# Half of the partial sums of three chunks: from an add on VectorE to a copy on ScalarE and an accumulating transfer

## The chip, the cores and the metric

The kernel runs on one core of a Trainium2 chip. The metric is the device time of one execution in microseconds; the time before is 965.22 us, the median of three runs (965.08 to 965.33). A profile was taken of one further execution of the same kernel. In views of the profile PE is TensorE (matmuls), PEld its weight load, DVE is VectorE, ACT ScalarE, POOL GpSimd and SP SyncE; an engine's name with a q is its queue, where transfers are issued.

## The reference

One encoder layer on 512 tokens of width 2048, all in float32. The part that matters here is the normalisation with a shift and a scale that depend on `c`, and the wide input projection:

```
mod = silu(c) @ w_ada + b_ada                  # 2048 -> 3 * 2048: shift, scale, gate
h = rms_norm(x, g) * (1 + scale) + shift       # 512 x 2048
proj = h @ w_in                                # 2048 -> 7168 columns
# proj is split into q, k, v, z of 8 attention heads and of 4 retention heads;
# attention (three dilated windows mixed), retention in both directions,
# both gated by silu(z), concatenated to y
out = rms_norm(x + gate * (y @ w_out), final_gain)
```

## The kernel before, in words

Every float32 product is made of three matmuls: each operand is split into a high part (a rounded copy, `hh` for h, `whi` for weights) and a low part (`hl`, `wlo`: the rest), and `mm3` (L89 to L92) adds high times high, low times high and high times low in PSUM. Of each piece of weights, ScalarE makes the high part (L173) and VectorE subtracts to get the low part (L178).

The input projection is cut into units of 256 columns. The shift and scale of a k tile (128 of the 2048 rows of h) need a full pass over 256 columns of `w_ada`, and that pass is long, so the first 13 units (phase 1) are not computed one after the other over all sixteen k tiles. The k tiles come in six chunks of 1, 2, 2, 3, 4 and 4 (`CHUNKS`, L36), and each chunk is multiplied into all 13 units as soon as its part of h is there. Two units (0 and 1) keep their PSUM banks (`pp`) through all chunks. The other eleven are "loose": in each chunk, each gets two banks `pw` of a pool of three (`psA`), and when its matmuls of this chunk are done, `post` (L945) takes the two banks out. The first time a unit is taken out, ScalarE copies the banks to the sums `acc` in SBUF (L952). Each later time VectorE adds them: `acc = acc + pw`, one instruction for each of the two banks (L954). The order of the units is turned round from chunk to chunk, and the last loose unit of a chunk keeps its banks and goes on as the first one of the next, so it isn't taken out at the turn. In chunks two, three and four that leaves 9, 10 and 10 units that are added.

Beside this, the next chunk's h is prepared in pieces (`ada_pieces`, L209): SP loads a block of `w_ada` (`araw`, three buffers, L223), VectorE adds it, weighted with silu(c), to `aacc` (L234; ScalarE does the first, L230), TensorE transposes the sum into a bank `psm` (L262), ScalarE adds it up along the row (`junk`, L267), three tiny VectorE instructions make shift and scale (L269 to L271), ScalarE makes `hh` and a float32 copy `ht` (L189, L193), and VectorE makes `hl` (L202). The pieces are handed out between the items of the current chunk. An item is loaded and converted ahead of its matmuls (`LEAD1` = 8 items for the load, `LOOK` = 2 for the conversion, three buffers each for `whi` and `wlo`). Weights and `w_ada` blocks are both issued by SP, in one queue. The first item of the later work on GpSimd is an iota at L491.

Each engine works its own list in order. The last chunk's `hh` tiles (k = 12 to 15) are made in chunk five; before that their SBUF is not used.

Of the kernel before, what the change touches and what calls it, by code (L numbers as in the profile page):

```python
# [9 lines left out]
F32 = mybir.dt.float32  # L10
F32R = mybir.dt.float32r
I32 = mybir.dt.int32
AF = mybir.ActivationFunctionType
ALU = mybir.AluOpType
# [3 lines left out]
P = 128  # L18
D = 2048
S = 512  # L20
NT = S // P
NK = D // P
# [13 lines left out]
CHUNKS = [1, 2, 2, 3, 4, 4]  # L36
# [14 lines left out]
def trunk_kernel(ctx, tc, x, c, norm_gain, w_ada, b_ada, w_in, w_out, dec_f, dec_b, final_gain, out):  # L51
    nc = tc.nc
# [10 lines left out]
    def bank(pool, nm):  # L63
        return pool.tile([P, 512], F32, tag="b", name=nm)
# [30 lines left out]
    c_row = const.tile([NK, P], F32, name="c_row")  # L95
    hp_scope = ExitStack()
    hp = hp_scope.enter_context(tc.tile_pool(name="hp", bufs=1, side="right"))
    hh = [hp.tile([P, S], F32R, name=f"hh{k}") for k in range(NK)]

    groups = [range(sum(CHUNKS[:i]), sum(CHUNKS[: i + 1])) for i in range(len(CHUNKS))]  # L100
    xt_tiles = {i: hp.tile([P, len(g), S], F32, tag=f"g{i}", name=f"xT{i}") for i, g in enumerate(groups) if i}
# [83 lines left out]

    def make_h(k, nk, k_first):
        tmp = aap.tile([P, S], F32, tag="ht", name="ht", bufs=4)
        a, b = av[:, k : k + 1], sv[:, k : k + 1]
        nc.scalar.activation(hh[k], xT[k], AF.Identity, scale=a, bias=b)  # L189
        if k_first == 1:  # L190
            nc.vector.tensor_scalar(tmp, xT[k], a, b, op0=ALU.mult, op1=ALU.add)
        else:
            nc.scalar.activation(tmp, xT[k], AF.Identity, scale=a, bias=b)  # L193
        tmps[k] = tmp
# [11 lines left out]
    def h_pieces(k0, nk):  # L206
        return [(lambda f=f, k=k: f(k, nk, k0)) for f in (make_h, make_hl) for k in range(k0, k0 + nk)]
# [350 lines left out]
    def shared_conv(c0s, k0, nk):  # L558
        m = len(c0s)
        lo_c = min(c0s)  # L560
        st = {}

        def ld():
            if k0 == 0 and lo_c == FIRST_W:
                assert m == 2
            elif "raw" not in st:
                raw = raw_tile()
                rv = raw[:, : nk * m * UC].rearrange("p (k f) -> p k f", k=nk)
                nc.sync.dma_start(
                    rv,  # L570
                    wi[k0 * P : (k0 + nk) * P, lo_c : lo_c + m * UC].rearrange("(k p) f -> p k f", p=P),
                )
                st["raw"] = rv

        def cv(j):
            off = (c0s[j] - lo_c) // UC
            if nk == 1:
                if k0 == 0 and lo_c == FIRST_W:
                    st[0] = first_w
                if off // 2 not in st:  # L580
                    a, b = off // 2 * 512, min(off // 2 * 512 + 512, m * UC)
                    st[off // 2] = conv(st["raw"][:, 0, a:b], b - a)
                w = st[off // 2]
                o = off % 2 * UC
                return w[0][:, o : o + UC], w[1][:, o : o + UC]
            return conv(st["raw"][:, :, off * UC : (off + 1) * UC], nk * UC)

        return [(ld, lambda j=j: cv(j)) for j in range(m)]
# [32 lines left out]
    def flush():  # L621
        while loaded or pending:
            feed(None)

    def unit_items(mode, c0, k0, nk, pss, start, stop, post, cvf=None):
        items = []
        hold = {}
        ks = list(range(k0, k0 + nk))
        for a in range(0, nk, 2):
# [16 lines left out]
            def mm(wt, kk=kk, last=(a + 2 >= nk)):  # L646
                if "ps" not in hold:
                    hold["ps"] = pss()
                ps = hold["ps"]
                wh = wt[0].rearrange("p (k f) -> p k f", f=UC)  # L650
                wl = wt[1].rearrange("p (k f) -> p k f", f=UC)
                if mode == "T":
                    for ft in range(2):
                        fs = slice(ft * P, (ft + 1) * P)
                        for j, k in enumerate(kk):
                            mm3(
                                ps[ft], wh[:, j, fs], wl[:, j, fs], hh[k], hl[k],
                                start and k == k0, stop and k == k0 + nk - 1, k == 0,
                            )
                else:  # L660
                    for t in range(NT):
                        o = ps[t // 2][:, (t % 2) * UC : (t % 2 + 1) * UC]
                        ts = slice(t * P, (t + 1) * P)
                        for j, k in enumerate(kk):
                            mm3(
                                o, hh[k][:, ts], hl[k][:, ts], wh[:, j, :], wl[:, j, :],
                                start and k == k0 and t % 2 == 0, stop and k == k0 + nk - 1,
                            )
                if last:
                    post(ps)  # L670
# [211 lines left out]
    def heads(g):  # L882
        return attention(2 * g, 0) + attention(2 * g + 1, 1)
# [6 lines left out]
    accs = {}  # L890
    begun = set()
    keep_now = {}
# [13 lines left out]
    def plan(fs, start, span):  # L906
        for i, f in enumerate(fs):
            agenda.setdefault(start + (i * span) // len(fs), []).append(f)
# [7 lines left out]
    def feed_next(item):  # L916
        nonlocal fed
        feed(item)
        fed += 1
        for f in agenda.pop(fed - 1, ()):  # L920
            f()

    for ci, nk in enumerate(CHUNKS):
        lastc = ci == len(CHUNKS) - 1
        early["on"] = ci < len(CHUNKS) - 2
        items = []
        order = ORDER
        if (len(CHUNKS) - 1 - ci) % 2:
            order = order[::-1]
        if lastc:  # L930
            order = list(range(NU))
        cvs = {}
        if nk <= 2:
            for g in GROUPS:
                per = 4 // nk
                for i in range(0, len(g), per):
                    part = g[i : i + per]
                    for u, f in zip(part, shared_conv([ph1[u][1] for u in part], k0, nk)):
                        cvs[u] = f
        loose = [u for u in order if u >= N_PERSIST]  # L940
        kept, keep_now = keep_now, {} if lastc else {loose[-1]: None}
        for u in order:
            mode, c0, ev = ph1[u]

            def post(ps, u=u, ev=ev, lastc=lastc, keep_now=keep_now):  # L945
                if u in keep_now:
                    keep_now[u] = ps
                    return
                if u >= N_PERSIST:
                    for i in range(2):  # L950
                        if u not in begun:
                            nc.scalar.copy(accs[u][i], ps[i])  # L952
                        else:
                            nc.vector.tensor_tensor(accs[u][i], accs[u][i], ps[i], op=ALU.add)  # L954
                    begun.add(u)
                if lastc:
                    src = accs[u] if u >= N_PERSIST else ps
                    if u < 4:
                        ev(src)
                    else:  # L960
                        queue.append(lambda: ev(src))
                    if u % 4 == 3:
                        queue.extend(heads(u // 4))

            if u < N_PERSIST:
                pss = lambda u=u: persist[u]
                start, stop = ci == 0, lastc
            elif u in kept:
                pss = lambda u=u, kept=kept: kept[u]
                start, stop = False, u not in keep_now  # L970
            else:
                pss = lambda: [bank(psA, "pw") for _ in range(2)]
                start, stop = True, u not in keep_now
            items += unit_items(mode, c0, k0, nk, pss, start, stop, post, cvs.get(u))
        if not lastc:
            n2 = CHUNKS[ci + 1]
            nxt = []
            for i in range(0, n2, 4):
                nxt += ada_pieces(k0 + nk + i, min(4, n2 - i))
            before_last = ci == len(CHUNKS) - 2  # L980
            span = int(len(items) * ADA_SPAN) if before_last else len(items)
            plan(nxt, fed + LAG, span)
            if before_last:
                agenda.setdefault(fed + LAG + span, []).append(open_wk)
        if ci == 0:
            for it in items:
                it["load"]()
        for it in items:
            feed_next(it)
        k0 += nk  # L990
# [299 lines left out]
    for t in range(NT):  # L1290
        ts = slice(t * P, (t + 1) * P)
        ps = bank(psP, "po")[:, :256]
# [30 lines left out]
```

## Time and profile before

| what | value |
|---|---|
| median of three runs | 965.22 us |
| the profiled execution | 967.67 us |
| its span (first to last instruction) | 965.9 us |
| PE busy over the span | 945.4 us |
| DVE busy over the span | 614.0 us |
| ACT busy over the span | 376.0 us |
| POOL busy over the span | 12.5 us |
| bytes moved by transfers | 141.49 MB |

"Busy" is the time in which an engine executes an instruction; an average over the span hides that the stages differ. So the profile is read by stretches of time: loose units of chunks two to four are added between 62 and 187 us of the span. A view of windows gives, for each stretch, the busy time of every engine, the granted TensorE clock (PEclk, 1.00 is full) and the share of the sixteen DMA engines that is busy. A view of waits says which engine stood still, at which line, until which other instruction ended: the total, the number of times and the longest.

### The profile page before, as it was taken

How to read it: one execution, taken by the hardware profiler on the slowest of the kernel's cores; microseconds unless marked ns; L12 is line 12 of the kernel's file. 1: busy time of each engine (PE TensorE's matmuls, PEld its weight loads, DVE VectorE, ACT ScalarE, POOL GpSimd, SP SyncE). 2: the span in 40 equal slices, each digit the busy share in tenths (PEclk: the TensorE clock that was granted, in tenths of full speed). 3: DMA queues.
4: the chain of work that ended last, by engine and by line, in shares of the span. 5: the costliest groups of instructions: out<-in, count | busy, mean ns of one | idle time of the engine just before them, and what ended most of it. 6: DMA issues, size and time to landing. Idle time of an engine off the chain costs nothing.

```text
span 965.9 us, 14382 instructions
## 1 busy us (share of the span) xinstructions
PE 945.4 (98%) x5602; PEld 821.6 (85%) x5602; DVE 614.0 (64%) x1076; ACT 376.0 (39%) x738; POOL 12.5 (1%) x25
## 2 busy tenths in 40 slices
PE   7999999999999999999999999999999999999996
PEld 6787688788888888988997899988899988888896
DVE  4899998949777876665456565745534382545444
ACT  4742425253254655544343232422333272333321
POOL 2000000000000000000000000000000000000001
PEclk9999999999999999999999999999999999999998
DMA  9997798424642222112225515436322147243304
GB/s 329 333 296 239 262 314 289 162 89 128 198 154 66 87 66 66 55 55 88 67 66 175 196 57 190 147 90 202 101 67 89 66 162 274 90 128 131 110 1 174
DMA packets 108947, 141.49 MB, mean 146 GB/s; under 512 B 5656, under 2 KB 78024, under 8 KB 108496
## 3 DMA queue, kind: packets, MB, share of 16 engines
q1 hardware_dynamic: 107200, 135.83, 43.5%
q10 hardware_dynamic: 1584, 4.72, 1.3%
q8 instruction: 44, 0.72, 0.3%
q14 instruction: 23, 0.19, 0.1%
q0 software_dynamic: 96, 0.03, 0.0%
HBM read 136.36 MB, written 4.20 MB: 146 GB/s over the span
## 4 chain that ended last, share of the span: by engine, by line
PE 82%; DMA 7%; DVE 6%; issue 2%; SPq 1%; ACT 1%; POOL 0%; POOLq 0%; DVEq 0%; ACTq 0%
PE pp L92 24%; PE pp L90 12%; PE po L92 12%; PE pw L92 11%; PE po L90 6%; PE pw L90 6%; PE op L92 3%; DMA araw<-in_w_ada_dram 3%; PE sp L92 2%; DMA graw<-in_w_ada_dram 2%; DVE aacc L234 2%; PE op L90 2%; PE tp L782 1%; DVE wlo L178 1%; SPq L117 1%
## 5 line engine op out<-in xcount | busy, mean ns | idle before, releaser
L173 ACT CAST whi<-raw 128x512 fp32r<-128x512 f32 (+1 forms) x289 | 175.1, 606 | 433.5 <-PE pp L92 203.1
L178 DVE TENSOR_TENSOR wlo<-raw,whi 128x512 fp32r<-128x512 f32 (+1 forms) x288 | 193.5, 672 | 208.3 <-ACT whi L173 201.8
L92 PE MATMUL pp<-wlo,hh 128*128 128x256 f32 x576 | 162.3, 282 | 0.5 <-DVE wlo L178 0.4
L90 PE MATMUL pp<-whi,hh 128*128 128x256 f32 x576 | 162.6, 282 | 0.0
L92 PE MATMUL pp<-whi,hl 128*128 128x256 f32 x576 | 161.6, 281 | 0.0
L90 PEld LDWEIGHTS pp<-whi,hh 128*128 128x128 f32 x576 | 108.5, 188 | 2.5 <-ACT sc L851 1.7
L92 PEld LDWEIGHTS pp<-wlo,hh 128*128 128x128 f32 x576 | 108.6, 189 | 1.9 <-DVE wlo L178 0.9
L92 PEld LDWEIGHTS pp<-whi,hl 128*128 128x128 f32 x576 | 108.6, 188 | 0.0
L90 PE MATMUL pw<-hh,whi 128*128 128x512 f32 x256 | 103.5, 404 | 3.6 <-ACT acc L952 1.9
L92 PE MATMUL pw<-hh,wlo 128*128 128x512 f32 x256 | 102.3, 400 | 0.8 <-DVE wlo L178 0.8
L90 PE MATMUL pp<-hh,whi 128*128 128x512 f32 x256 | 102.0, 398 | 0.4 <-DVE kl L682 0.4
L92 PE MATMUL pw<-hl,whi 128*128 128x512 f32 x256 | 102.0, 398 | 0.0
L92 PE MATMUL pp<-hh,wlo 128*128 128x512 f32 x256 | 101.2, 397 | 0.0
L92 PE MATMUL pp<-hl,whi 128*128 128x512 f32 x256 | 101.2, 395 | 0.0
L92 PE MATMUL po<-wlo,yh 128*128 128x512 f32 (+1 forms) x252 | 92.7, 368 | 0.0
L92 PE MATMUL po<-whi,yl 128*128 128x512 f32 (+1 forms) x252 | 92.6, 368 | 0.0
L90 PE MATMUL po<-whi,yh 128*128 128x512 f32 (+1 forms) x252 | 92.6, 367 | 0.0
L234 DVE SCALAR_TENSOR_TENSOR aacc<-araw,ct,aacc 128x512 f32<-128x512 f32 (+2 forms) x75 | 76.0, 1015 | 6.7 <-ACT aacc L230 3.8
L954 DVE TENSOR_TENSOR acc<-acc,pw 128x512 f32<-128x512 f32 x100 | 67.0, 684 | 8.0 <-PE pw L92 7.6
L1007 DVE SCALAR_TENSOR_TENSOR gacc<-graw,ct,gacc 128x512 f32<-128x512 f32 x60 | 45.0, 750 | 40.9 <-DMA graw<-in_w_ada_dram 40.7
L90 PEld LDWEIGHTS pw<-hh,whi 128*128 128x128 f32 x256 | 48.5, 190 | 19.1 <-DVE acc L954 4.9
L90 PEld LDWEIGHTS pp<-hh,whi 128*128 128x128 f32 x256 | 48.1, 188 | 13.4 <-ACT e L727 0.9
(234 smaller groups left out, 1559.3 us busy)
## 6 DMA issues: line engine op xcount, KB each, us to landing
raw<-in_w_in_dram SPq DMA_DIRECT2D x94, 512.0 KB, 3.7
araw<-in_w_ada_dram SPq DMA_DIRECT2D x48, 512.0 KB, 6.7
graw<-in_w_ada_dram SPq DMA_DIRECT2D x64, 256.0 KB, 2.9
raw<-in_w_out_dram SPq DMA_DIRECT2D x32, 512.0 KB, 3.7
raw<-in_w_in_dram SPq DMA_DIRECT2D x16, 384.0 KB, 4.2
araw<-in_w_ada_dram SPq DMA_DIRECT2D x16, 384.0 KB, 4.9
res<-in_x_dram SPq DMA_DIRECT2D x16, 256.0 KB, 6.2
raw<-in_w_in_dram SPq DMA_DIRECT2D x11, 256.0 KB, 5.8
```

What stands on the lines that cost most here:

```text
L90: nc.tensor.matmul(o, lh, rh, start=start, stop=False, skip_group_check=True)
L92: nc.tensor.matmul(o, a, b, start=False, stop=stop and b is (rl if swap else rh), skip_group_check=True)
L117: q.dma_start(raw0[b][:, i * 8 : (i + 1) * 8], wa[i * 8 * P : (i + 1) * 8 * P, b * D : b * D + P].rearrange("(a p) f -> p a f", p=P),)
L173: c1 = nc.scalar.copy(dh, src)
L178: c2 = nc.vector.tensor_tensor(dl, src, f32(dh), op=ALU.subtract)
L234: ins = nc.vector.scalar_tensor_tensor(acc[:, :, :n], rv[:, a], ct[:, kr + a : kr + a + 1], acc[:, :, :n], op0=ALU.mult, op1=ALU.add,)
L782: nc.tensor.transpose(tp_[:, j * P : (j + 1) * P], pt[:, j * P : (j + 1) * P], ident)
L954: nc.vector.tensor_tensor(accs[u][i], accs[u][i], ps[i], op=ALU.add)
L1007: nc.vector.scalar_tensor_tensor(st["acc"], raw, ct[:, kr : kr + 1], st["acc"], op0=ALU.mult, op1=ALU.add)
```

## The change

In chunks two, three and four, a loose unit that has been taken out before has its first bank added by VectorE as before, and its second bank treated otherwise: ScalarE copies it to a tile `part` in SBUF, and GpSimd issues a transfer from `part` to `acc` that adds to what is there. Chunks one, five and six are as before. The four buffers of `part` take the places in SBUF of the last chunk's four `hh` tiles, which are allocated when they are made instead of at the start.

```
-    hh = [hp.tile([P, S], F32R, name=f"hh{k}") for k in range(NK)]
+
+    LAST = NK - CHUNKS[-1]
+    hh = [hp.tile([P, S], F32R, name=f"hh{k}") for k in range(LAST)] + [None] * (NK - LAST)
+    n_part = [0]
+
+    def part_tile():
+        n_part[0] += 1
+        return hp.tile([P, S], F32, tag=f"hp{LAST + n_part[0] % (NK - LAST)}", name="part")
...
     def make_h(k, nk, k_first):
         tmp = aap.tile([P, S], F32, tag="ht", name="ht", bufs=4)
+        if k >= LAST:
+            hh[k] = hp.tile([P, S], F32R, tag=f"hp{k}", name=f"hh{k}")
...
-            def post(ps, u=u, ev=ev, lastc=lastc, keep_now=keep_now):
+            def post(ps, u=u, ev=ev, lastc=lastc, keep_now=keep_now, by_dma=0 < ci < len(CHUNKS) - 2):
...
                         if u not in begun:
                             nc.scalar.copy(accs[u][i], ps[i])
+                        elif i == 1 and by_dma:
+                            part = part_tile()
+                            nc.scalar.copy(part, ps[i])
+                            nc.gpsimd.dma_start(accs[u][i], part, accum_op=ALU.add)
                         else:
                             nc.vector.tensor_tensor(accs[u][i], accs[u][i], ps[i], op=ALU.add)
```

## Prediction

> **What bounds the kernel now.** I read the page's first part, then the windows over the stretch that the change touches, then groups and waits in that stretch, then the order of single instructions where TensorE stood still.
>
> ```profile
> span 965.9 us, 14382 instructions
> ...
> PE 945.4 (98%) x5602; PEld 821.6 (85%) x5602; DVE 614.0 (64%) x1076; ACT 376.0 (39%) x738; POOL 12.5 (1%) x25
> ```
>
> Over the span TensorE is the bound: 20.5 us of 965.9 are without a matmul. Whatever the change does, it can win only from those 20.5 us, and only from the part of them in its stretch. The windows (columns: length, then busy time and count for PE, PEld, DVE, ACT, POOL, then clock, DMA share, GB/s) show that stretch, first in pieces, then whole, then the one behind it:
>
> ```profile
> 62.00:77.00 15.00, 14.39 (x78) 11.45 (x76) 14.20 (x26) 8.01 (x18) 0.00 (x0) 1.00 0.83 273
> 77.00:104.00 27.00, 24.71 (x101) 18.30 (x101) 26.05 (x36) 6.83 (x15) 0.00 (x0) 1.00 0.80 266
> 104.00:126.00 22.00, 21.82 (x129) 18.88 (x130) 21.53 (x33) 9.51 (x21) 0.00 (x0) 1.00 0.74 228
> 126.00:140.00 14.00, 14.00 (x64) 11.32 (x63) 12.72 (x14) 3.32 (x7) 0.00 (x0) 1.00 0.97 341
> 140.00:187.00 47.00, 46.22 (x254) 39.17 (x253) 43.51 (x65) 19.37 (x47) 0.00 (x0) 1.00 0.75 252
> 62.00:187.00 125.00, 121.13 (x621) 99.13 (x620) 118.01 (x172) 47.03 (x105) 0.00 (x0) 1.00 0.79 263
> 187.00:260.00 73.00, 72.94 (x388) 61.69 (x388) 54.55 (x105) 25.83 (x55) 0.88 (x1) 1.00 0.42 132
> ```
>
> From 62 to 187 us VectorE is busy for 118.0 of 125 us, as full as TensorE at 121.1; ScalarE has 78 us free and GpSimd everything. But a full VectorE is not yet a loss: TensorE misses only 125 - 121.1 = 3.9 us here. The waits of this stretch (total us, times, longest) say what TensorE and its weight load stood still for:
>
> ```profile
> PEld pw L90 <- DVE acc L954: 4.4, 9, 1.8
> ACT aacc L230 <- DMA araw<-in_w_ada_dram: 3.4, 3, 1.3
> ...
> PEld psm L262 <- ACT junk L267: 2.5, 3, 1.3
> ...
> DVE aacc L234 <- DMA araw<-in_w_ada_dram: 2.4, 4, 1.2
> ...
> PE psm L262 <- ACT junk L267: 1.4, 2, 0.8
> PE pw L90 <- DVE acc L954: 1.3, 1, 1.3
> PEld pw L92 <- DVE wlo L178: 1.2, 1, 1.2
> ...
> PE pw L92 <- DVE wlo L178: 0.8, 1, 0.8
> ```
>
> Two kinds: matmuls that wait for VectorE (a bank not yet emptied by L954, a low part not yet made by L178), and transposes of the sums that wait for ScalarE (L267). The first kind is what the change can remove.
>
> **The change, part by part.**
>
> *VectorE loses 29 adds.* The groups of VectorE in the stretch (count | busy us, mean ns):
>
> ```profile
> L234 DVE SCALAR_TENSOR_TENSOR aacc<-araw,ct,aacc 128x1024 f32<-128x1024 f32 (+2 forms) x48 | 55.4, 1154 | 4.3 <-DMA araw<-in_w_ada_dram 2.4 <-ACT aacc L230 1.7
> L954 DVE TENSOR_TENSOR acc<-acc,pw 128x512 f32<-128x512 f32 x58 | 38.4, 683 | 0.2
> L178 DVE TENSOR_TENSOR wlo<-raw,whi 128x512 fp32r<-128x512 f32 (+1 forms) x48 | 29.4, 615 | 0.5 <-ACT whi L173 0.3
> ```
>
> 58 adds are 29 units with two banks, which is 9 + 10 + 10. Half go: 29 x 0.683 = 19.8 us, and VectorE falls from 118.0 to 98.2 us. It stops being the bound of the stretch. What TensorE gets from that is not 19.8 us but the waits of the first kind. The weight load runs ahead of the matmul in progress, so a wait of the load costs less than its length. This shows at the longest one:
>
> ```profile
> 96.81 0.39 PE L92 MATMUL pw<-hl,whi 128*128 128x512 f32 x1
> 97.04 0.40 PE L92 MATMUL pw<-hh,wlo 128*128 128x512 f32 x1
> 98.77 0.50 PE L90 MATMUL pw<-hh,whi 128*128 128x512 f32 x1 [1.33 <-DVE acc L954]
> ```
>
> Unhindered matmuls of this shape start 0.23 us apart; here it is 1.73, a loss of 1.50, where the load waited 1.8. So I take the ten waits of the load, 4.4 + 1.2 = 5.6 us, less 0.23 for each: 5.6 - 2.3 = **3.3 us**. The bounds are 2.1 (the two waits of matmuls alone, 1.3 + 0.8) and 5.6. With VectorE at 98.2 of some 122 us I expect all of it to go. What is late next is the transposes that wait for ScalarE, and they stay. Behind 187 us TensorE is at 72.94 of 73, so time won before is handed on to the end.
>
> *ScalarE gets 29 copies.* A copy of a bank to SBUF and ScalarE's main group in the stretch:
>
> ```profile
> L952 ACT COPY acc<-pw x22: 575/588/623, 30.3 to 60.1; 128x512 f32<-128x512 f32 x22
> ```
> ```profile
> L173 ACT CAST whi<-raw 128x512 fp32r<-128x512 f32 (+1 forms) x48 | 26.8, 561 | 71.5 <-PE pw L92 58.3 <-PE pp L92 8.3 <-DVE acc L954 2.5
> ```
>
> 29 x 0.588 = 17.1 us, to 64 of 122: ScalarE does not become the bound. The copy adds a wait: it cannot start before the unit's last matmul. Behind it stands the next `whi`, but that one waits for the same matmuls now (58.3 us of its 71.5) to get its buffer, and is made two items, 5.6 us, ahead; 0.6 us later does no harm. Where it does harm is the chain of sums: `junk` can come behind a copy, and TensorE waits for `junk`. That is at most 0.59 us at each of the three chunk preparations in the stretch, 1.8 in all, and at least nothing (ScalarE stands idle for `araw` right ahead of them, 3.4 us in three times, and a copy fits in there). I take one of the three, **0.6 us**.
>
> *GpSimd gets 29 issues.* Nothing else is on its queue in the stretch. Before and after it:
>
> ```profile
> 1.25 0.67 POOL L122 DMA_DIRECT2D c_row<-in_c_dram  x1 [0.81 <-POOLq L1312]
> ...
> 2.63 0.54 POOL L145 DMA_DIRECT2D bg_row<-in_b_ada_dram  x1
> ...
> 220.67 0.88 POOL L491 IOTA tabs<- 128x896 int32 x1 [196.43 <-ACT whi L173]
> ```
>
> An issue of a small transfer takes it 0.5 to 0.7 us, and one is due per unit: 12 matmuls at 0.23, 2.8 us, in chunks two and three, 4.2 in chunk four. Even at three times 0.67 it keeps up. The iota comes 30 us later than the last issue. The issue waits for the copy and, for a sum whose earlier transfer is still under way, for that one too; at the turn of two chunks these are three units, 8.4 us, apart. What waits behind it on GpSimd is only the next issue. The last chunk's `hh` tiles take the `part` buffers in chunk five, behind the stretch: nothing.
>
> *The transfers.* The trace has no accumulating transfer. Its nearest rows are the load queue in the stretch, transfers of the same 256 KB in a quiet and in a full stage, and the one queue of GpSimd, in the full stage at the start (last number: us to landing):
>
> ```profile
> q1 hardware_dynamic: 22109, 32.80, 78.9%
> ...
> raw<-in_w_in_dram SPq DMA_DIRECT2D x5, 256.0 KB, 2.8
> ```
> ```profile
> res<-in_x_dram SPq DMA_DIRECT2D x16, 256.0 KB, 6.2
> ...
> c_row<-in_c_dram POOLq DMA_DIRECT2D x1, 8.0 KB, 5.8
> ```
>
> The loads take 78.9% of 125 us, 98.6 us of all sixteen engines, for 32.8 MB: 3.0 us per MB, 0.79 us for 0.262 MB. If an accumulate costs one such pass, 29 take 22.9 us and the engines are needed for 121.5 us of about 122: just full. If it costs two (it has two inputs), 45.8 and 144.4: over by 22. Below one pass it can't be by these rows, since the bytes must move at least once. I take one pass, which is nearest to the rows (a transfer of this size as it is), and no loss to TensorE from it: 126 to 140 us of the trace has the engines at 0.97 and TensorE at 14.00 of 14.00, so a full set of engines is survivable while blocks of `w_ada` come only a little late.
>
> The Trainium skill speaks against the change here. Its page "DMA: Bandwidth & Descriptors" says, under "Issuing engines are not separate DMA queues", that transfers of whatever engine run on the same sixteen DMA engines and only the issue time is saved; under "Rules for kernel authors" that an accumulate reads its destination and writes it later. With the page's ceiling of 435 GB/s (section "Specifications") two reads of 29 tiles would be an estimated 35 us, and the sum 134 of 122. No row of this trace can show either; half of the 12 us over, charged as in the second rival below, would make it 968.5.
>
> *Sum.* -3.3 + 0.6 = -2.7 us. The profiled execution took 967.67 us, so the sum for it is 965.0. It stood 2.45 above the median of 965.22; I apply the difference to the median: 962.5.
>
> **The rivals.**
>
> *Nothing that can be told.* A difference of 0.2%, 1.9 us, is about what a measurement of this kernel can tell from none. The gain of 3.3 shrinks under that if ScalarE's place in the sums costs all of its 1.8 us, and its three waits for the first `araw` block (3.4 us) grow by a third, 1.1, since a copy that stands behind them now holds up a bank of TensorE: -3.3 + 1.8 + 1.1 = -0.4, 964.8. For it: those waits exist today, in the very stretch. Against: VectorE frees `araw` buffers sooner, so the loads are asked for sooner.
>
> *The DMA engines become the bound (the other side).* Place: 66 to 187 us, where blocks of `w_ada` come late, VectorE stands still at L234 with low parts and adds queued behind it, and transposes on TensorE wait for the sums. It decides from about one pass per transfer (0.79 us). At two passes 22 us are over. VectorE has then 24 us of idle time to absorb late blocks, and the next stretch has 58% of the DMA engines free, 42 us; so between nothing and 22 reaches TensorE, and I take half: -2.7 + 11 = +8.3, 973.5. For it: the DMA share of 0.79, with pieces at 0.97, and two inputs per addition. Against: TensorE was unhurt where they were full, and it was VectorE, not the transfers, that held these loads back in SP's queue (waits of SP, 50 to 260 us):
>
> ```profile
> SPq L223 <- DVE aacc L234: 27.9, 14, 5.2
> ```
>
> *Four buffers are too few.* ScalarE stands still at its copy until a `part` buffer has been read out, and with it everything behind. Four units are 11.2 us; less 0.6 for the copy and 0.7 for the issue, a transfer may take 9.9 us. At 2.8 to 6.2 it doesn't matter. At twice 6.2 a round takes 13.7 us, a unit 3.4 instead of 2.8, and 19 units of chunks two and three lose 11.8: 965.2 - 2.7 + 11.8 = 974.3. Against it: the landing must be twice that of the full stage.
>
> **How the numbers follow.** Forecast, VectorE's waits go and the transfers are hidden: 0.42, with its own range from 959.6 (all 5.6 us) to 963.3. No difference that can be told: 0.27. DMA engines the bound: 0.25. Buffers: 0.06. Faster is thus 0.42, same 0.27, slower 0.31. The range goes from 959.6 to 974, which takes in the prices of the rivals; outside lie accumulates at over two passes and gains beyond VectorE's waits, together less than 2 in 10. It is lopsided since the gain is capped by named waits and the loss isn't.
>
> **What the changed profile would show.** Right: in the stretch 29 adds at L954 (in 58's place), VectorE below 85%, the waits of matmuls for L954 and L178 near zero, 29 copies of about 0.59 us, landings of the accumulates under 9 us, and the same order of matmuls with chunk five beginning about 3 us sooner. Wrong: DMA share near 1.0 over the whole stretch with long waits at L234 and L230 for `araw`, or at the transposes for the sums (DMA rival); ScalarE's copies waiting for transfers (buffers); waits of L262 for `junk` grown as much as those for L954 shrank (no difference).

## The result, and the profile after

The changed kernel takes 978.68 us (median of four runs, 977.4 to 979.9) against 965.15 (the kernel before, now four runs): a ratio of 1.0136, 95% interval 1.0119 to 1.0154. It is 1.4% slower, where 962.5 with a range up to 974 was predicted. Its profiled execution took 977.4 us and has a span of 975.6, 9.7 us more than the span before. That is less than the 13.5 us between the medians, because the profiled execution before lies 2.5 us above its median and this one 1.3 us below its own.

The page's first part:

```profile
span 975.6 us, 14450 instructions
...
PE 946.9 (97%) x5602; PEld 822.7 (84%) x5602; DVE 598.3 (61%) x1047; ACT 389.6 (40%) x767; POOL 37.9 (4%) x54
```

VectorE's busy time fell by 15.7 us and 29 instructions, and the kernel is slower. First: where? TensorE's matmuls for the adaLN gate (`psg`) come at a fixed place in the later work. Before, after, and in the first experiment below, without the transfers (the two times are the first and the last start):

```profile
L1015 PE MATMUL psg<-gacc,ones x8: 590/591/592, 508.0 to 709.6; 128*1 128x512 f32 x8
```
```profile
L1029 PE MATMUL psg<-gacc,ones x8: 590/590/591, 518.3 to 719.5; 128*1 128x512 f32 x8
```
```profile
L1028 PE MATMUL psg<-gacc,ones x8: 590/591/592, 503.6 to 704.7; 128*1 128x512 f32 x8
```

508.0 has become 518.3 and 709.6 has become 719.5: the whole loss lies ahead of 508 us and none is added behind; without the transfers the same place comes 4.4 us sooner than before. The windows of the changed stretch:

```profile
62.00:77.00 15.00, 15.00 (x81) 12.55 (x80) 12.64 (x21) 10.32 (x24) 4.39 (x5) 1.00 1.06 300
77.00:104.00 27.00, 22.57 (x86) 17.20 (x85) 20.33 (x28) 7.36 (x16) 5.22 (x6) 0.87 1.09 322
104.00:126.00 22.00, 21.85 (x124) 18.54 (x123) 19.45 (x27) 15.02 (x34) 6.19 (x8) 1.00 1.06 291
126.00:140.00 14.00, 11.93 (x53) 9.53 (x52) 6.61 (x8) 1.88 (x5) 0.79 (x1) 0.88 1.07 337
140.00:187.00 47.00, 42.51 (x235) 35.30 (x234) 39.32 (x54) 22.39 (x53) 6.10 (x7) 1.00 0.96 301
62.00:187.00 125.00, 113.87 (x572) 93.12 (x571) 98.35 (x136) 56.97 (x127) 22.69 (x26) 0.96 1.03 308
```

VectorE's 98.35 us looks like the 98.2 of the prediction, but that is luck. The changed kernel gets through less work in these 125 us: VectorE has 136 instructions in them, where 172 - 29 would be 143. Over the whole span 29 adds fewer are worth 15.7 us of busy time, 0.54 each, not 19.8. Instructions that follow each other closely overlap in the record, as the last two of VectorE's lines below show: the first starts at 131.22 and takes 1.28, the next starts at 132.42.

TensorE misses 125 - 113.9 = 11.1 us instead of 3.9, and the DMA engines' share went from 0.79 to 1.03. A share above 1 means that the recorded times of packets overlap; it says that the engines are full, not by how much. The waits from 62 to 200 us name the new bound:

```profile
DVE aacc L244 <- DMA araw<-in_w_ada_dram: 20.5, 12, 5.3
...
PE pw L90 <- DVE acc L968: 4.0, 1, 4.0
...
PE pw L92 <- DVE wlo L186: 3.2, 4, 1.4
...
PE pp L92 <- DVE wlo L186: 2.1, 1, 2.1
PE pw L90 <- ACT whi L181: 1.7, 1, 1.7
```

VectorE waits 20.5 us for blocks of `w_ada`, where it was 2.4, and behind it in its queue stand the low parts and the adds for which TensorE then waits. One such place, in VectorE's order:

```profile
124.63 1.28 DVE L244 SCALAR_TENSOR_TENSOR aacc<-araw,ct,aacc 128x1024 f32<-128x1024 f32 x1
131.22 1.28 DVE L244 SCALAR_TENSOR_TENSOR aacc<-araw,ct,aacc 128x1024 f32<-128x1024 f32 x1 [5.31 <-DMA araw<-in_w_ada_dram]
132.42 0.68 DVE L186 TENSOR_TENSOR wlo<-raw,whi 128x512 fp32r<-128x512 f32 x1
```

The low part at 132.42 is the one for which TensorE stands still 2.07 us until 133.16. What filled the engines (queues between 62 and 200 us: packets, MB, share of sixteen engines), and the copies and issues:

```profile
q1 hardware_dynamic: 21988, 32.59, 67.9%
q0 software_dynamic: 4176, 7.60, 30.9%
```
```profile
L965 ACT COPY part<-pw x29: 566/584/606, 62.4 to 195.2; 128x512 f32<-128x512 f32 x29
L966 POOL DMA_DIRECT2D acc<-part x29: 863/872/932, 63.3 to 196.1; - x29
```

30.9% of 138 us are 42.6 us for 29 accumulates: 1.47 us of all sixteen engines each. The prediction took a single pass, at 0.79. The price does not come from the engines being full: from 187 to 200 us the engines are at 0.63 in all, and three accumulates take 34.5% of these 13 us there, 1.5 us each.

### The profile page after: what moved, and what is told of

The parts are those of the page before. It is cut to its first block, busy times and chain, and to the rows that moved or that the text cites. A ratio compares the mean times of both kernels' runs of the same rounds, so it can differ in the third digit from the quotient of the medians.

```text
span 975.6 us, 14450 instructions
## 1 busy us (share of the span) xinstructions
PE 946.9 (97%) x5602; PEld 822.7 (84%) x5602; DVE 598.3 (61%) x1047; ACT 389.6 (40%) x767; POOL 37.9 (4%) x54
## 4 chain that ended last, share of the span: by engine, by line
PE 82%; DMA 9%; DVE 4%; SPq 2%; issue 1%; ACT 1%; POOL 0%; DVEq 0%; POOLq 0%; ACTq 0%
PE pp L92 23%; PE pw L92 13%; PE po L92 12%; PE pp L90 12%; PE pw L90 6%; PE po L90 6%; DMA araw<-in_w_ada_dram 6%; PE op L92 3%; DMA graw<-in_w_ada_dram 2%; PE sp L92 2%; DVE aacc L244 2%; PE op L90 2%; PE tp L792 1%; SPq L125 1%; PE sp L90 1%
## 5 line engine op out<-in xcount | busy, mean ns | idle before, releaser
L244 DVE SCALAR_TENSOR_TENSOR aacc<-araw,ct,aacc 128x512 f32<-128x512 f32 (+2 forms) x75 | 76.1, 1015 | 25.0 <-DMA araw<-in_w_ada_dram 20.5
L92 PEld LDWEIGHTS pp<-hh,wlo 128*128 128x128 f32 x256 | 48.5, 189 | 14.5 <-DVE wlo L186 2.8
L92 PEld LDWEIGHTS pw<-hh,wlo 128*128 128x128 f32 x256 | 48.7, 190 | 14.0 <-DVE wlo L186 2.6
```

Of the source, the lines that this page charges most:

```text
L92: nc.tensor.matmul(o, a, b, start=False, stop=stop and b is (rl if swap else rh), skip_group_check=True)
L244: ins = nc.vector.scalar_tensor_tensor(acc[:, :, :n], rv[:, a], ct[:, kr + a : kr + a + 1], acc[:, :, :n], op0=ALU.mult, op1=ALU.add,)
```

## The experiments

Theory: the accumulates cost the DMA engines about two passes each, the engines are full between 62 and 187 us, and the blocks of `w_ada` come late. Rivals: ScalarE's copies hold up its queue (rival S); issue, landing or order of GpSimd's transfers cost by themselves, whatever else the engines do (rival G). The kernel before was timed beside each group: 965.66, 966.25 and 965.84 us.

**No transfer at all.** The 29 second banks are copied and not added.

```
                             nc.scalar.copy(part, ps[i])
-                            nc.gpsimd.dma_start(accs[u][i], part, accum_op=ALU.add)
```

> The changed kernel without its 29 transfers: ScalarE still copies each second bank to the part tile, and nobody adds it (29 of the partial sums are left out of the result). If the sixteen DMA engines are what costs the time, VectorE's relief shows unspoiled: 961 to 963 us, the waits of VectorE for araw near the 2.4 us of the kernel before. If ScalarE's copies in its order cost the time, 975 us or more, as with the transfers.

961.64 us, 0.9956 of before (0.9942 to 0.997). In its window from 62 to 187 us, and its wait for `araw`:

```profile
62.00:187.00 125.00, 122.83 (x633) 102.03 (x633) 105.03 (x145) 62.08 (x136) 0.00 (x0) 1.00 0.79 265
```
```profile
DVE aacc L244 <- DMA araw<-in_w_ada_dram: 6.2, 7, 1.8
```

All the copies are there and the time is lower than before: rival S falls. (VectorE's wait for `araw` is 6.2 us, not near the 2.4 that was expected.) VectorE's relief is worth 4 us when the DMA engines stay at 0.79; the transfers take that and 13 us more, 17 in all.

**A plain copy instead of the accumulate**, on the same queue with the same waits.

```
-                            nc.gpsimd.dma_start(accs[u][i], part, accum_op=ALU.add)
+                            nc.gpsimd.dma_start(accs[u][i], part)
```

> The same 29 transfers on GpSimd's queue, between the same tiles and with the same waits, but as a plain copy that overwrites the sum (so 29 partial sums are wrong). If the accumulate costs the DMA engines a second pass for reading its destination, their time for GpSimd's queue falls from 43 us (4.4% of the span) to some 23, and the loss shrinks by about half or more: 964 to 971 us. If issue, queue and landing on GpSimd are what costs, nothing changes: 977 to 980.

968.28 us, 1.0022 (1.0007 to 1.0036). GpSimd's queue in the stretch of 125 us:

```profile
q0 software_dynamic: 2283, 7.52, 15.5%
```

15.5% are 19.4 us, 0.67 each, under half of an accumulate, with 2283 packets for the same bytes where the accumulate has 4176 in its 138 us. Against the kernel without transfers the plain copies cost 6.6 us, the accumulates 17. Rival G, which expected no change, falls as the whole cause. But the plain copies aren't free either. The stretch with them:

```profile
62.00:187.00 125.00, 120.82 (x624) 99.53 (x623) 104.74 (x144) 60.48 (x134) 15.95 (x29) 1.00 0.92 324
```

At a share of 0.92, still under one on average, the transfers already take back all that VectorE's relief brings.

**The same plain copies, issued by ScalarE.**

```
-                            nc.gpsimd.dma_start(accs[u][i], part, accum_op=ALU.add)
+                            nc.scalar.dma_start(accs[u][i], part)
```

> The 29 transfers as plain copies (the sums are overwritten), issued by ScalarE instead of GpSimd. If only the time on the sixteen DMA engines counts, the same as the plain copies of GpSimd's queue, 965 to 970 us. If GpSimd's queue has a price of its own, 961 to 964.

970.18 us, 1.0051 (1.0038 to 1.0064). Its queue:

```profile
q10 hardware_dynamic: 4032, 7.34, 15.9%
```

The same share of the engines and no gain from another queue: GpSimd's queue shows no price of its own. With 4032 packets, nearly as many as the accumulates have, a plain copy still costs 15.9%, 19.9 us: the number of packets doesn't make the accumulate dear. (The value lies just outside the 965 to 970 of the theory. In its trace TensorE waits once for 2.5 us for a low part, and its granted clock over the stretch is 0.97 where the plain copies of GpSimd's queue have 1.00; whether the queue has to do with that is not shown.)

**Half of the loads away, the accumulates as they are.** Every second block of `w_ada` isn't loaded, and the one before is used again (shift and scale are wrong).

```
+            if kr // npc % 2:
+                raws[kr] = raws[kr - npc]
+                return
             raw = aap.tile([P, 2048], F32, tag="araw", name="araw", bufs=AR)
```

> The changed kernel with its accumulating transfers, but only every second block of w_ada is loaded and each loaded one is used twice (shift and scale are wrong). The other side of the same account: if the DMA engines are full, freeing them of half these blocks brings the time to 960 to 964 us with 29 accumulates in place. If the accumulates' landing, order or issue is the cause, it stays at 975 to 980.

967.62 us, 1.0014 (1.0004 to 1.0025). Queues, and ScalarE's wait for `araw`, from 62 to 187 us:

```profile
q1 hardware_dynamic: 14269, 19.63, 47.5%
q0 software_dynamic: 4026, 7.34, 34.3%
```
```profile
ACT aacc L243 <- DMA araw<-in_w_ada_dram: 9.8, 2, 5.1
```

With the same 29 accumulates, but the engines at 0.82, 11 us of the loss are gone. The 960 to 964 expected were not reached: the edit also moved the first block of the next chunk ahead in ScalarE's order, and ScalarE waits 9.8 us for it in two places. That may be the rest; no run shows it apart.

**Fewer and more accumulates.** Odd units only (13 transfers over the three chunks), chunk two only (9), chunk four only (10), and both banks (58). The first four lines are cut from the line of `def post`:

```
-by_dma=0 < ci < len(CHUNKS) - 2
+by_dma=0 < ci < len(CHUNKS) - 2 and u % 2     # odd units
+by_dma=ci == 1                                # chunk two
+by_dma=ci == 3                                # chunk four
...
-                        elif i == 1 and by_dma:
+                        elif by_dma:                          # both banks
```

> Accumulating transfers for the odd units only, about half of the 29; the even units are added by VectorE. If the loss comes from filling the DMA engines, it has a threshold: 98.6 us of loads and some 21 us of accumulates are about the 122 us that there are, so less than a third of the loss is left, 963 to 970 us. If each transfer costs by itself (issue, landing, order), half the loss stays: 971 to 973.

> The 9 accumulates of chunk two only (62 to 87 us of the span). The DMA engines are at 0.8 there, and the nine ask for 13 us in 25: over for a while, and behind it the loads can catch up in part. DMA theory: 964 to 970 us. A cost for each transfer by itself would give a third of the loss, 969 to 970.

> The 10 accumulates of chunk four only (from some 150 us on). Loads take 0.75 of the DMA engines there and end at its end; ten accumulates ask for 15 us in 45, which about fits, and the stretch behind it is at 0.42. DMA theory: 963 to 967 us. A cost for each transfer by itself: 969 to 970.

> Both banks of the 29 units go by copy and accumulating transfer, 58 in all. The account of the DMA engines: 98.6 us of loads and 58 x 1.48 = 86 us, 184 of 122 us. If time over that account comes out one to one beyond what the 29 cost, the 43 us more bring 1010 to 1030 us. If each transfer costs by itself, the loss against the kernel without transfers (17 us for 29) doubles: 993 to 998.

| accumulates | time, us | ratio to before (95%) |
|---|---|---|
| 13, spread (odd units) | 968.35 | 1.0024 (1.0013 to 1.0035) |
| 9, chunk two | 970.21 | 1.0048 (1.0032 to 1.0065) |
| 10, chunk four | 968.82 | 1.0028 (1.0015 to 1.0040) |
| 29 | 978.68 | 1.0136 (1.0119 to 1.0154) |
| 58 | 1013.41 | 1.0483 (1.0465 to 1.0501) |

Thirteen spread over three chunks cost no more than nine in chunk two alone (their intervals just overlap), and the second 29 cost 35 us where the first cost 17: what counts is how many fall into a time that has room for few. In the last kernel, between 62 and 225 us:

```profile
q1 hardware_dynamic: 20810, 31.37, 57.3%
q0 software_dynamic: 7486, 13.63, 45.8%
```
```profile
DVE aacc L244 <- DMA araw<-in_w_ada_dram: 59.0, 16, 11.8
ACT part L965 <- DMA acc<-part: 29.4, 24, 2.8
```

The engines are at 1.03 for the whole of a stretch that has grown, and now ScalarE, too, waits for `part` buffers, which it never did with 29; some of the 35 us may come that way. A price for each transfer by itself would have given 993 to 998 here and 971 to 973 for the thirteen. The two single chunks don't decide between the accounts: chunk two only lies at the upper end of both (964 to 970, and 969 to 970). Chunk four only is the value that fits worst: 2.6 us slower than before where the account said up to 1 us and a price for each transfer some 3. Its engines are at 0.87 from 140 to 200 us, so some of that loss is not explained by the sum over a stretch.

**The add elsewhere: on GpSimd, or later on VectorE.**

```
-                            nc.gpsimd.dma_start(accs[u][i], part, accum_op=ALU.add)
+                            nc.gpsimd.tensor_tensor(accs[u][i], accs[u][i], part, op=ALU.add)   # one kernel
+                            nc.vector.tensor_tensor(accs[u][i], accs[u][i], part, op=ALU.add)   # the other
```

> No transfer: GpSimd adds the part tile to the sum itself. If the DMA engines are the cause, the loss is gone and the gain forecast is there, 961 to 964 us, provided that GpSimd's add takes less than a unit (2.8 us) and doesn't slow VectorE, whose adds and subtractions keep their 0.68 us. If ScalarE's copies are the cause, 975 or more.

> ScalarE copies the second bank to the part tile as in the change, and VectorE adds the tile from SBUF; no transfer. VectorE's work is that of the kernel before, ScalarE's that of the change. If the DMA engines are the cause: 962 to 966 us, since nothing is added to them, and the banks come free a little sooner. If ScalarE's copies in its order cost more than 2 us: 967 or more.

GpSimd's adds: 979.96 us, 1.0138 (1.0119 to 1.0156), no better than the transfers and for another reason. GpSimd needs 1.48 us for an add, but VectorE stretches beside it (GpSimd's add, then VectorE at the time when three of them run):

```profile
76.40 4.71 POOL L966 TENSOR_TENSOR acc<-acc,part 128x512 f32<-128x512 f32 x3 [3.55 <-ACT part L965]
```
```profile
76.49 1.78 DVE L212 TENSOR_TENSOR hl<-ht,hh 128x512 fp32r<-128x512 f32 x1
78.20 3.45 DVE L186 TENSOR_TENSOR wlo<-raw,whi 128x512 fp32r<-128x512 f32 x2
81.58 0.67 DVE L968 TENSOR_TENSOR acc<-acc,pw 128x512 f32<-128x512 f32 x1
```

A subtraction with both inputs in SBUF takes 1.78 us there, alone it took 0.69; the add with one input in PSUM keeps its 0.67. The Trainium skill has this rule on the page "SBUF — State Buffer", "Who interferes with whom": a VectorE instruction with two SBUF inputs contends with a GpSimd instruction that reads SBUF. The trace agrees. In the changed kernel VectorE isn't slowed like this: its adds at L244 take 1015 ns on average over the span, as they did before.

VectorE's own add from the copy: 965.07 us, 0.999 (0.998 to 1.0001), not told apart from before. With the copies of the change and none of its transfers nothing is lost, which clears ScalarE a second time; and nothing is won while VectorE keeps the work. None of the kernels that do the whole computation is clearly faster than the kernel before.

## Why the prediction was wrong, point by point

- *VectorE loses 29 adds*: the mechanism is right. Its busy time fell by 15.7 us where 19.8 was expected, and without the transfers the kernel is 4 us faster than before, where the term had 3.3 with bounds of 2.1 to 5.6, and the sum 2.7.
- *ScalarE gets 29 copies*: right. 0.584 us each, no loss from them.
- *GpSimd gets 29 issues*: right. 0.87 us each, above the 0.67 of its row, and it keeps up.
- *The transfers*: here the step failed that took one pass, "nearest to the rows", at "no loss to TensorE". An accumulate measured 1.47 us of the sixteen engines, twice the 0.67 of a plain copy of the same tile, and the account went from "just full" to 98.6 + 42.6 = 141 us of 122. The prediction had the number: its upper bound, two passes and 45.8 us, is close to the 42.6 measured, and it named the two inputs and what the Trainium skill's page "DMA: Bandwidth & Descriptors" says of them under "Rules for kernel authors", that an accumulate reads its destination and writes it later. The run with plain copies agrees with that rule by its price; that the second pass is that read is not shown by itself.
- *No loss to TensorE from one pass*: this failed too, apart from the price. The plain copies are one pass, measured at 0.67 us, and cost 6.6 us: that kernel takes 968.28 us, outside the 959.6 to 963.3 that the forecast gave for hidden transfers.
- *The rival with full DMA engines* is what happened, at the place and by the waits that it named. It was given 0.25, and its price was halved because idle time on VectorE and a free stretch behind would absorb the rest. They don't: idle time of an engine helps only if the wait falls where nothing is queued behind it. The transfers cost 17 us; the rival had 22 over and charged 11.
- *That TensorE was unhurt at a share of 0.97* (126 to 140 us) was read as slack. It was slack that could be spent once: with the engines full from 62 us on, the same stretch lost 2.1 us, and some more by the clock (below).
- *Four buffers are too few*: no. The accumulates landed in 6.7 us in the median; ScalarE waited for buffers only with 58.

## What to carry to other kernels

A transfer that adds is not a transfer of the same size: count what it reads as well as what it writes, and where the trace doesn't show it, let two inputs mean two passes. Before work is moved from a full engine to "free" DMA, add it to the share of the DMA engines in that very stretch; at 0.79 there was no room for 29 tiles of 256 KB in 125 us. And price a full engine by what it takes from the path (here VectorE: all busy, yet only some 4 us of waits), not by its busy time.

## What the runs showed of the hardware that was not expected

After a stall TensorE can go on at half speed. Matmuls behind the wait of 4 us in the changed kernel, and two windows there (the last three numbers are the granted clock, the DMA share and GB/s):

```profile
97.29 0.80 PE L90 MATMUL pw<-hh,whi 128*128 128x512 f32 x1 [4.02 <-DVE acc L968]
97.88 0.63 PE L92 MATMUL pw<-hl,whi 128*128 128x512 f32 x1
98.31 0.63 PE L92 MATMUL pw<-hh,wlo 128*128 128x512 f32 x1
```
```profile
98.00:99.00 1.00, 1.00 (x4) 0.81 (x3) 1.00 (x3) 0.00 (x0) 0.00 (x0) 0.50 1.11 238
...
103.00:104.00 1.00, 1.00 (x8) 0.81 (x7) 0.50 (x1) 0.30 (x3) 0.00 (x0) 1.00 1.15 295
```

Starts are 0.43 us apart instead of 0.23 at a clock of 0.50, until 103 us. So the stall cost about 4 us by itself and some 2.5 more behind it, which no wait in the profile shows. The shorter stall at 133.16 does the same:

```profile
133.16 0.50 PE L92 MATMUL pp<-hh,wlo 128*128 128x512 f32 x1 [2.07 <-DVE wlo L186]
133.84 0.63 PE L92 MATMUL pp<-hl,whi 128*128 128x512 f32 x1
134.26 0.63 PE L92 MATMUL pp<-hh,wlo 128*128 128x512 f32 x1
```

Until 137.1 us starts are 0.43 us apart here too, which costs some 1.6 us. The two together are 4 us, beside the 7.2 us that TensorE misses more than before; that is about the 10.3 us by which the gate comes later. The Trainium skill's page "TensorE: Matmul & The Clock Gate" ("What's actually happening") says that the clock is halved after an idle window of about 3.4 us and comes back after as long a busy one. The trace agrees with the second (5.3 and 3.9 us of matmuls until full clock), and with the first only for the stall of 4.02 us: 2.07 us were enough at 133 us. Nor does such a stall always do it. At 31 us both kernels wait for ScalarE, the one before for 1.93 us and the changed one for 1.92; behind it, from 32 to 34 us, the clock is 0.50 in the profiled execution before and 1.00 in the one after. What decides this is not shown.
